# Where a layer's side work is done: sums of output-weight quarters, modulation columns and pauses regrouped between stages of a two-layer backbone

## The chip, the cores and the metric

The kernel runs on one core of a Trainium2 chip. The metric is device time in microseconds (us) of one launch; several launches of the same program are summarised by their median. A profile is of one execution, whose own time stands beside it.

## What is computed

Two layers over 2048 latent tokens of width 1024 in fp32. Layer 0 is a chunked gMLP, layer 1 a multi-scale pooling mixer; the third kind of layer does not occur, and the context tokens are not used. Cut to what matters here:

```python
for i in range(2):
    shift, scale, gate = split(silu(c) @ ada_w[i] + ada_b[i], 3)      # the modulation: 24 columns of 128
    h = rmsnorm(x, norm_g[i]) * (1 + scale) + shift
    if i == 0:
        u, v, g = split(h @ w_in, 3)
        v = layernorm(gelu(v)); s = per-group 128x128 mix of v + b_s   # the spatial gate
        y = (gelu(u) * s * silu(g)) @ w_out
    else:
        p, g = split(h @ w_in, 2)
        y = (group-mixed (centred mean(p) - p) * scale * silu(g)) @ w_out
    x = x + gate * y
return rmsnorm(x, final_g)
```

## The kernel before, in words

**Matrix products.** Every fp32 product is made of three matmuls (`mm3`, lines 105 to 109) on operands split into a high and a low part: ScalarE rounds the high part, VectorE subtracts it (`put`, lines 111 to 114). Larger products use a seven-product scheme on 2x2 blocks, so that weights and activations also have to be added and subtracted block by block. A `Stream` (lines 33 to 60) lists all weight jobs in order: SyncE's queue loads them, `make` splits them, and a consumer keeps three or four pairs made ahead of the one it takes (`st.ahead`).

**Stages.** The span is: fusing two weights of layer 1 (7 to 115 us); then, for each half of the tokens of layer 0, the phase of the values v (`v_phase`, lines 821 to 875; the gate values of the spatial gating), the phase of the units u and gate (`b_phase0`, 927 to 963: eight c, each with a u unit and a gate unit of seven products, and four spatial mixes between), and the output product (`c_pairs` by `c_phase0`, 975 to 1013); then layer 1 with `b_phase1` (1131 to 1163), `c_pairs` again, `b_phase1`, and a last output product. In what follows V(0), B0(0), C0(0), V(1), B0(1), C0(1), B1(0) are these phases in order.

**Side work.** Work that no product of the phase needs at once is a list of small steps in one queue, `side`. `do_side(n)` (118 to 120) runs the next n. `v_phase` calls it after each of its 56 tiles of 12 matmuls: two steps after each of the first eight tiles when it is V(0), one otherwise (line 867). `b_phase0` has 112 calls, one after each product (12 matmuls); `pace` (931 to 933) divides what is left by the calls that are left and rounds up. `b_phase1` runs one step after each product of a first unit and two after each product of a gate unit (line 1161); its own pooling steps go in ahead of the rest. The order of instructions of each engine is fixed when the program is built, by program order and by the builder's own estimate of when each can start; `load` (128 to 131) puts a side load into SyncE's queue behind the stream's last load.

**The side work that the diff touches.**
- `sum_quarters(dst, q)` (732 to 751): `fetch` issues four loads of 256 KB on GpSimd's queue into the tiles x, x, ra, th; `sums` does four subtractions on VectorE (lines 744 to 747; the first is held in program order) and issues four stores on GpSimd's queue. x has two buffers, ra and th one each, so a fetch waits for the stores before. `spaced` (753) makes it fetch, rest, rest, sums, rest: five steps, eight times. `tsum_o` sums the quarters of layer 0's output weight into `to_d`, `tsum` those of layer 1's fused weight into `t_d`, `tsum_p` those of layer 1's output weight into `tp_d`.
- `ada_late(i, *gs)` (468 to 470): for each g four columns of the modulation of layer i, in 14 steps: a first load, eight steps of one 256 KB load into x (SyncE's queue) and one multiply-add on VectorE into ra (lines 452, 454), four rests, and `last`, four small products on TensorE (`pm`, line 460) that need ra. Columns 0 to 15 are shift and scale, 16 to 23 gate.
- `fetched_rms(..., wait)` (544 to 567): eight squares summed over 1024 rows into ra, then `wait` rests, `root` (`pss`, line 502), `wait` rests, `diagonals`, `wait` rests, `spread` (`pr`, line 526): 12 + 3·wait steps.
- `bias_steps` and `late[1]` (769, 818): 12 and 4 steps at the start of V(0).

Where each is needed: `to_d` in C0(0) and C0(1); `tp_d` and layer 1's gate columns in layer 1's first output product; layer 1's shift and scale in C0(1), where B1(0)'s rows are made.

Of the kernel before, what the change touches and what calls it, by code (L numbers as in the profile page):

```python
# [22 lines left out]
TB = 512  # L23
# [40 lines left out]
def hybrid_kernel(ctx: ExitStack, tc: tile.TileContext, a: dict):  # L64
# [29 lines left out]
    def work(tag, width=512):  # L94
        return wk.tile([P, WK[tag][0]], F32, name=tag, tag=tag, bufs=WK[tag][1])[:, 0:width]

    def bank(name="ps"):
        return ps.tile([P, 512], F32, name=name, tag="ps")
# [15 lines left out]
        nc.vector.tensor_sub(pair[1], src, pair[0].bitcast(F32))  # L114

    side = deque()

    def do_side(n=1000):
        for _ in range(min(n, len(side))):
            side.popleft()()  # L120
# [7 lines left out]
    def load(dst, src):  # L128

        with tc.issue_after(st.last):  # L130
            nc.sync.dma_start(dst, src)
# [291 lines left out]
    def ahead(n, fetch, places=2):  # L423

        got = []

        def get(i):
            while len(got) < min(n, i + 1 + places):
                got.append(fetch(len(got)))
            return got[i]  # L430

        return get

    def ada_steps(i, g0, ng, raw, acc_tile):

        box = []
        cols = slice(g0 * P, (g0 + ng) * P)

        def fetch(k):
            r = raw()[:, 0:ng * P]  # L440
            load(r, a["ada_w"][i, k, :, cols])
            return r

        row = ahead(KD, fetch, 1)

        def step(k):
            if k == 0:
                box.append(acc_tile())
            acc = box[0][:, 0:ng * P]
            r = row(k)  # L450
            if k == 0:
                nc.vector.tensor_scalar_mul(acc, r, cond[:, 0:1])
            else:
                nc.vector.scalar_tensor_tensor(acc, r, cond[:, k:k + 1], acc, ALU.mult, ALU.add)

        def last():
            acc = box[0]
            pm = bank("pm")
            for m in range(ng):
                nc.tensor.matmul(pm[:, m:m + 1], acc[:, m * P:(m + 1) * P], ones[:, 0:1], start=True, stop=True)  # L460
            s = slice(g0, g0 + ng)
            nc.vector.tensor_add(mod[i][:, s], pm[:, 0:ng], ada_b[i][:, s])
            if g0 < 16 <= g0 + ng:
                nc.vector.scalar_tensor_tensor(acol[i], mod[i][:, KD:2 * KD], 1.0, norm_g[i], ALU.add, ALU.mult)

        return [partial(row, 0)] + [partial(step, k) for k in range(KD)] + [last]

    def ada_late(i, *gs):
        return [f for g in gs for t in (ada_steps(i, g, 4, lambda: work("x"), lambda: work("ra")),)
                for f in t[:-1] + [rest] * 4 + t[-1:]]  # L470
# [67 lines left out]
    def src0(b):  # L538
        return lambda d: a["xT"][d, :, b * TB:(b + 1) * TB]

    def src1(b):
        return lambda d: x1_d[d, :, b * TB:(b + 1) * TB]

    def fetched_rms(src, n, acc, sq, wait=0, kept=None):

        rms = Rms(n, acc, sq)

        def fetch(d):
            x = work(sq if kept is None else "g", n)
            load(x, src(d))  # L550
            if kept is not None:
                kept.append(x)
            return x

        row = ahead(KD, fetch, 1)

        def step(d):
            x = row(d)
            if d == 0 or kept is not None:
                rms.square(x, d == 0)  # L560
            else:
                nc.scalar.activation(x, x, AF.Square)
                nc.vector.tensor_add(rms.acc, rms.acc, x)

        pause = [lambda: None] * wait
        return rms, ([partial(row, 0)] + [partial(step, d) for d in range(KD)] + pause
                     + [rms.root] + pause + [rms.diagonals] + pause + [rms.spread])
# [4 lines left out]
    class Rows:  # L572
# [9 lines left out]
        def fetch(self, half, d, tile_of):  # L582
            x = tile_of()
            load(x, self.src[half](d))
            return x
# [167 lines left out]
    def spaced(jobs):  # L753
        return [g for fetch, sums in jobs for g in (fetch, rest, rest, sums, rest)]
# [14 lines left out]
    def bias_steps():  # L769

        box = []

        def fetch(q):
            box[:] = [work(tag) for tag in ("x", "x", "ra", "th")]
            nc.gpsimd.dma_start(box[2], a["w_sT"][:, q * 512:q * 512 + 512])
            nc.gpsimd.dma_start(box[3], a["b_s"][:, q * 512:q * 512 + 512].broadcast_to([P, 512]))

        def make(q):
            wsT, bsb = box[2:]
            pw = bank("pw")  # L780
            nc.tensor.matmul(pw, ones, wsT, start=True, stop=True)
            for i in range(2):
                for g in range(2):
                    for h in range(2):
                        c, o = 2 * (4 * q + 2 * i + g) + h, (2 * i + g) * P
                        nc.vector.scalar_tensor_tensor(
                            box[i][:, (2 * g + h) * P:(2 * g + h + 1) * P], pw[:, o:o + P], vb[:, c:c + 1],
                            bsb[:, o:o + P], ALU.mult, ALU.add)
                nc.gpsimd.dma_start(bt_d[4 * q + 2 * i:4 * q + 2 * i + 2].rearrange("g p n -> p g n"),
                                    box[i].rearrange("p (g n) -> p g n", g=2))  # L790

        return [f for q in range(2) for f in (partial(fetch, q), rest, rest, partial(make, q), rest, rest)]
# [6 lines left out]
    rms, steps = fetched_rms(src0(1), TB, "ra", "x", 0, others)  # L799
    rms0.append(rms)  # L800
    late = rows.rest_steps(xb, others)
# [124 lines left out]

    def b_phase0(bb, rows, stats):
        st.ahead = 4
        left = [112]

        def pace():
            left[0] -= 1
            return -(-len(side) // (left[0] + 1))

        fetch, normalise, mix = spatial(bb, stats)
        fetch(0)
        normalise(0)
        for c in range(8):
            gu = [work("g") for _ in range(4)]
            u = unit(rows, jug[bb][c][0], gu, lambda j: nc.scalar.activation(gu[j], gu[j], AF.Gelu_apprx_tanh))  # L940
            for i, pn in enumerate(ORDER):
                u(pn, pace())
                if i == 3:
                    ss = mix(c)
            for j in (0, 2, 3, 1):
                nc.vector.tensor_mul(ss[j], ss[j], gu[j])
            gt = [work("g") for _ in range(4)]

            def gate(j):
                nc.scalar.activation(gt[j], gt[j], AF.Silu)  # L950
                nc.vector.tensor_mul(ss[j], ss[j], gt[j])
                if j != 2:
                    nc.gpsimd.dma_start(y_d[bb, c, (0, 1, None, 3)[j]], ss[j])

            g = unit(rows, jug[bb][c][1], gt, gate)
            for i, pn in enumerate(ORDER):
                g(pn, pace())
                if c < 7 and i == 0:
                    fetch(c + 1)
                if c < 7 and i == 3:  # L960
                    normalise(c + 1)
            side.appendleft(partial(row_sums, bb, c, ss, gt))
        do_side()
# [53 lines left out]
    tsum_p = [sum_quarters(tp_d[k], lambda h, k=k: a["p_wo"][k + 8 * h]) for k in range(8)]  # L1017
    tsum_o = [sum_quarters(to_d[k], lambda h, k=k: a["g_wo"][2 * k + h]) for k in range(8)]


    side.extend(late[1] + bias_steps())
    stats = v_phase(0, rows)
    do_side()
    rms0 = []
    for b in (2, 3):
        rms, steps = fetched_rms(src0(b), TB, "ra", "x", 5)
        rms0.append(rms)
        side.extend(steps)
    side.extend(spaced(tsum_o) + ada_late(0, 16, 20) + ada_late(1, 0, 4, 8))
    b_phase0(0, rows, stats)  # L1030
    rows = Rows(0, [src0(2), src0(3)], rms0)
    sums = rows.sum_steps(lambda: work("g"))
# [7 lines left out]
    do_side()  # L1040
    rms1 = []
    for b in (0, 1):
        rms, steps = fetched_rms(src1(b), TB, "ra", "x", 8)
        rms1.append(rms)
        side.extend(steps)
    side.extend(spaced(tsum_p) + ada_late(1, 12, 16, 20))
    b_phase0(1, rows, stats)
    rows = Rows(1, [src1(0), src1(1)], rms1)
    sums = rows.sum_steps(lambda: work("g"))
# [119 lines left out]
    b_phase1_side = []  # L1169
    rms1 = []  # L1170
    for b in (2, 3):
        rms, steps = fetched_rms(src1(b), TB, "ra", "x", 8)
        rms1.append(rms)
        b_phase1_side += steps
    side.extend(b_phase1_side)
    b_phase1(0, rows)

    rows = Rows(1, [src1(2), src1(3)], rms1)
# [30 lines left out]
    for j, (t0, n) in enumerate(LAST):  # L1209
# [3 lines left out]
        rms = Rms(n, "ra", "x")  # L1213
# [79 lines left out]
```

## Time and profile before

| what | value |
|---|---|
| median of 3 launches | 2444.57 us (2443.26 to 2446.61) |
| the profiled execution's own time | 2441.26 us |
| span in its profile | 2439.5 us |
| TensorE (matmul) busy | 2375.7 us, 97% |
| VectorE busy | 1985.2 us, 81% |
| ScalarE / GpSimd busy | 1091.8 us, 45% / 402.6 us, 17% |
| mean granted TensorE clock | 0.986 |
| mean DMA traffic | 198 GB/s |

The profile cuts the span into 40 slices of 61 us and gives the busy share of each engine in each, the clock that TensorE was granted as a share of 2.4 GHz, and the share of the 16 DMA engines. Other views of the same execution give windows of one's own choice, the instructions of one engine in order of time, who waited for whom, and the chain of work that ended last. Times in them are us from the span's start. In a row of instructions the arrow reads output<-input, and what stands in brackets is the engine's idle time just before and what ended it.

### The profile page before, as it was taken

The numbers are of one execution on the slowest core, as the hardware profiler recorded it, in microseconds if no ns is written. First come the engines' busy times: TensorE is split into PE (matmuls) and PEld (weight loads), VectorE is DVE, ScalarE is ACT, GpSimd is POOL, SyncE is SP. The second block draws the span as 40 slices with busy tenths as digits, with TensorE's granted clock in tenths as the row PEclk, the third lists the DMA queues.
The fourth block names the chain that finished last, engine by engine and source line by source line (L and its number), as shares of the span: only waits on it lengthen the run. The fifth ranks groups of instructions, "written<-read, shape, count | busy, mean of one in ns | idle before, by whom it ended". The sixth has DMA issues, their size and how long they took to land.

```text
span 2439.5 us, 33346 instructions
## 1 busy us (share of the span) xinstructions
PE 2375.7 (97%) x11104; PEld 2000.2 (82%) x11104; DVE 1985.2 (81%) x3323; ACT 1091.8 (45%) x1886; POOL 402.6 (17%) x742
## 2 busy tenths in 40 slices
PE   8999999599999999999999999999999999999998
PEld 7768888488888887888788788888888888888998
DVE  6885887789888786887998878899889688988655
ACT  5743553244465344543445553333356433323533
POOL 2211114300101342014211011121111101000011
PEclk9999999799999999999999999999999999999999
DMA  9733446754678775448657775443378735446764
GB/s 373 248 125 116 159 142 236 241 189 158 209 266 271 242 248 195 142 152 267 232 180 255 245 252 169 138 150 130 120 241 261 252 132 181 142 131 188 225 193 131
DMA packets 204765, 483.41 MB, mean 198 GB/s; under 512 B 27168, under 2 KB 52768, under 8 KB 203568
## 3 DMA queue, kind: packets, MB, share of 16 engines
q1 hardware_dynamic: 152784, 314.00, 40.3%
q0 software_dynamic: 47776, 162.52, 18.9%
q10 hardware_dynamic: 4032, 4.75, 0.7%
q8 instruction: 88, 1.44, 0.3%
q14 instruction: 85, 0.70, 0.1%
HBM read 356.47 MB, written 124.70 MB: 197 GB/s over the span
## 4 chain that ended last, share of the span: by engine, by line
PE 67%; DMA 7%; DVE 5%; issue 4%; POOL 1%; ACT 0%; SPq 0%; POOLq 0%; DVEq 0%; ACTq 0%
PE pu L107 14%; PE pu L109 13%; PE pu L108 13%; PE po L109 7%; PE po L107 7%; PE po L108 7%; DVE wlo L114 2%; PE psp L907 1%; PE pa L109 1%; PE pa L108 1%; PE pa L107 1%; DMA x<-in_g_wo 1%; DMA raw<-to_d 1%; DMA x<-x_d 1%; DMA raw<-in_g_wo 1%
## 5 line engine op out<-in xcount | busy, mean ns | idle before, releaser
L113 ACT CAST whi<-raw 128x512 fp32r<-128x512 f32 (+1 forms) x960 | 562.9, 617 | 596.2 <-PE pu L108 225.8
L114 DVE TENSOR_TENSOR wlo<-raw,whi 128x512 fp32r<-128x512 f32 (+1 forms) x960 | 631.7, 683 | 127.9 <-ACT whi L113 125.0
L107 PE MATMUL pu<-S,whi 128*128 128x512 f32 x1024 | 403.4, 394 | 14.7 <-DVE g L695 8.1
L109 PE MATMUL pu<-S,wlo 128*128 128x512 f32 x1024 | 401.2, 392 | 0.7 <-DVE wlo L114 0.7
L108 PE MATMUL pu<-S,whi 128*128 128x512 f32 x1024 | 401.0, 392 | 0.0
L107 PE MATMUL pu<-A,whi 128*128 128x512 f32 x768 | 301.8, 393 | 0.0
L109 PE MATMUL pu<-A,wlo 128*128 128x512 f32 x768 | 300.0, 391 | 0.0
L108 PE MATMUL pu<-A,whi 128*128 128x512 f32 x768 | 299.8, 390 | 0.0
L109 PE MATMUL po<-whi,wlo 128*128 128x512 f32 (+1 forms) x672 | 262.6, 391 | 3.5 <-DVE wlo L114 3.4
L107 PE MATMUL po<-whi 128*128 128x512 f32 (+1 forms) x672 | 261.8, 390 | 0.0
L108 PE MATMUL po<-wlo,whi 128*128 128x512 f32 (+1 forms) x672 | 261.6, 389 | 0.0
L107 PEld LDWEIGHTS pu<-S,whi 128*128 128x128 f32 x1024 | 193.7, 189 | 55.8 <-DVE g L695 9.3
L109 PEld LDWEIGHTS pu<-S,wlo 128*128 128x128 f32 x1024 | 193.6, 189 | 42.2 <-DVE wlo L114 1.6
L108 PEld LDWEIGHTS pu<-S,whi 128*128 128x128 f32 x1024 | 193.9, 189 | 39.6
L109 PEld LDWEIGHTS pu<-A,wlo 128*128 128x128 f32 x768 | 144.7, 188 | 30.6
L108 PEld LDWEIGHTS pu<-A,whi 128*128 128x128 f32 x768 | 145.0, 189 | 29.8
L107 PEld LDWEIGHTS pu<-A,whi 128*128 128x128 f32 x768 | 145.1, 189 | 29.6
L109 PEld LDWEIGHTS po<-whi,wlo 128*128 128x128 f32 x672 | 126.1, 188 | 33.2 <-DVE wlo L114 7.3
L108 PEld LDWEIGHTS po<-wlo,whi 128*128 128x128 f32 x672 | 126.2, 188 | 26.5
L107 PEld LDWEIGHTS po<-whi 128*128 128x128 f32 x672 | 126.2, 188 | 26.0
L107 PE MATMUL po<-big,whi 128*128 128x388 f32 (+1 forms) x384 | 123.2, 321 | 0.0
L108 PE MATMUL po<-big,whi 128*128 128x388 f32 (+1 forms) x384 | 122.8, 320 | 0.0
(261 smaller groups left out, 4075.6 us busy)
## 6 DMA issues: line engine op xcount, KB each, us to landing
raw<-in_p_wo SPq DMA_DIRECT2D x120, 256.0 KB, 3.5
raw<-y_d SPq DMA_DIRECT2D x112, 256.0 KB, 3.7
v_d<-g POOLq DMA_DIRECT2D x64, 256.0 KB, 3.0
raw<-in_g_wu SPq DMA_DIRECT2D x32, 512.0 KB, 4.4
raw<-in_g_wg SPq DMA_DIRECT2D x32, 512.0 KB, 4.4
raw<-v_d SPq DMA_DIRECT2D x32, 512.0 KB, 4.7
y_d<-s POOLq DMA_DIRECT2D x64, 256.0 KB, 3.3
x<-in_ada_w SPq DMA_DIRECT2D x64, 256.0 KB, 3.3
```

The lines of the kernel that those rows point to most:

```text
L107: nc.tensor.matmul(out, w[0], x[0], start=first and not onto, stop=False, skip_group_check=onto)
L108: nc.tensor.matmul(out, w[0], x[1], start=False, stop=False, skip_group_check=onto)
L109: nc.tensor.matmul(out, w[1], x[0], start=False, stop=last, skip_group_check=onto)
L113: nc.scalar.copy(pair[0], src)
L114: nc.vector.tensor_sub(pair[1], src, pair[0].bitcast(F32))
L907: nc.tensor.matmul(p[:, t * P:(t + 1) * P], vt[h][:, t * 2 * P + j * P:t * 2 * P + (j + 1) * P], bw[:, 0:P], start=True, stop=True)
```

## The change

The closure `pace` becomes a function `evenly`, with the same arithmetic. `tsum_o` (40 steps) goes from B0(0) to V(0), behind the 16 steps that were there. Of the modulation of layer 1, columns 8 to 11 go from B0(0) to B0(1), and columns 16 to 23 from B0(1) to B1(0). The four `fetched_rms` for layer 1's rows that ran with pauses of 8 rests get 5.

```diff
+    def evenly(places):
+
+        left = [places]
+
+        def pace():
+            left[0] -= 1
+            return -(-len(side) // (left[0] + 1))
+
+        return pace
...
     def b_phase0(bb, rows, stats):
         st.ahead = 4
-        left = [112]
-
-        def pace():
-            left[0] -= 1
-            return -(-len(side) // (left[0] + 1))
-
+        pace = evenly(112)
...
-    side.extend(late[1] + bias_steps())
+    side.extend(late[1] + bias_steps() + spaced(tsum_o))
     stats = v_phase(0, rows)
...
-    side.extend(spaced(tsum_o) + ada_late(0, 16, 20) + ada_late(1, 0, 4, 8))
+    side.extend(ada_late(0, 16, 20) + ada_late(1, 0, 4))
     b_phase0(0, rows, stats)
...
     for b in (0, 1):
-        rms, steps = fetched_rms(src1(b), TB, "ra", "x", 8)
+        rms, steps = fetched_rms(src1(b), TB, "ra", "x", 5)
...
-    side.extend(spaced(tsum_p) + ada_late(1, 12, 16, 20))
+    side.extend(spaced(tsum_p) + ada_late(1, 8, 12))
     b_phase0(1, rows, stats)
...
     for b in (2, 3):
-        rms, steps = fetched_rms(src1(b), TB, "ra", "x", 8)
+        rms, steps = fetched_rms(src1(b), TB, "ra", "x", 5)
...
-    side.extend(b_phase1_side)
+    side.extend(b_phase1_side + ada_late(1, 16, 20))
     b_phase1(0, rows)
```

Steps per phase, by counting the lists (without the eight `row_sums` of a B0 phase, which are put in front): V(0) 16 before and 56 after, B0(0) 164 and 110, B0(1) 154 and 122, B1(0) 72 and 82 (beside its own pooling and gating steps).

## Rows read from the trace of the kernel before

**Rows 1.** The page, busy tenths and granted clock in 40 slices of 61 us

```profile
PE   8999999599999999999999999999999999999998
PEclk9999999799999999999999999999999999999999
```

**Rows 2.** Windows of B0(0), B0(1), B1(0), V(0), V(1): PE, PEld, DVE, ACT, POOL, clock, DMA, GB/s

```profile
278.49:658.20 379.71, 350.06 (x1668) 293.25 (x1666) 316.42 (x549) 153.68 (x251) 68.11 (x120) 0.96 0.58 189
966.94:1313.42 346.48, 342.07 (x1652) 288.14 (x1650) 307.38 (x538) 151.05 (x253) 69.49 (x122) 0.99 0.59 197
1470.42:1778.99 308.57, 308.57 (x1378) 256.02 (x1377) 273.16 (x422) 105.82 (x179) 54.46 (x136) 1.00 0.46 146
...
114.93:278.65 163.72, 158.21 (x678) 127.22 (x677) 125.39 (x217) 82.29 (x143) 29.65 (x42) 0.99 0.39 129
811.99:967.10 155.11, 153.45 (x674) 126.09 (x673) 111.54 (x184) 68.95 (x119) 58.04 (x99) 1.00 0.68 227
```

**Rows 3.** Window of 20 us inside B0(0), same columns

```profile
460.00:480.00 20.00, 5.28 (x24) 4.04 (x22) 17.39 (x31) 2.40 (x4) 3.79 (x7) 0.69 0.69 233
```

**Rows 4.** Timeline of PE: start, us, engine, line, out<-in, idle before and its end

```profile
431.26 0.79 PE L107 MATMUL pu<-S,whi 128*128 128x512 f32 x1 [6.55 <-DVE g L690]
...
483.91 0.59 PE L460 MATMUL pm<-ones,ra 128*128 128x1 f32 x2 [18.63 <-DVE ra L454]
...
1161.98 0.79 PE L107 MATMUL pu<-S,whi 128*128 128x512 f32 x1 [4.41 <-DVE g L695]
```

**Rows 5.** Chain that ended last, B0(0): start, us, what

```profile
424.25 7.59 DMA to_d<-x
...
432.40 3.80 DMA x<-in_g_wo
...
466.52 3.98 DMA x<-in_ada_w
```

**Rows 6.** Timeline of DVE: first and last of eight first subtractions in B0(0), V(1), B0(1)

```profile
372.36 0.68 DVE L744 TENSOR_TENSOR x<-x 128x512 f32<-128x512 f32 x1
...
460.32 0.69 DVE L744 TENSOR_TENSOR x<-x 128x512 f32<-128x512 f32 x1 [1.91 <-DMA x<-in_g_wo]
...
820.65 0.69 DVE L744 TENSOR_TENSOR x<-x 128x512 f32<-128x512 f32 x1 [2.69 <-issue]
...
920.21 0.69 DVE L744 TENSOR_TENSOR x<-x 128x512 f32<-128x512 f32 x1 [6.15 <-issue]
...
1088.44 0.68 DVE L744 TENSOR_TENSOR x<-x 128x512 f32<-128x512 f32 x1
...
1190.31 0.68 DVE L744 TENSOR_TENSOR x<-x 128x512 f32<-128x512 f32 x1
```

**Rows 7.** Chain that ended last, later in B0(0): the modulation's small products

```profile
530.30 0.79 PE pm L460 x8
...
572.93 0.79 PE pm L460 x8
```

**Rows 8.** Modulation steps, 484 to 658 us: duration min/median/max; then their waits: total, times, longest

```profile
L454 DVE SCALAR_TENSOR_TENSOR ra<-x,cond,ra x28: 737/744/752, 489.4 to 639.3; 128x512 f32<-128x512 f32 x28
...
DVE ra L454 <- DMA x<-in_ada_w: 2.1, 3, 0.8
```

**Rows 9.** Windows: early V(0), what follows, V(1) to 930 us, c = 4 to 6 of B1(0)

```profile
135.00:155.00 20.00, 15.88 (x58) 11.71 (x59) 19.78 (x39) 7.25 (x11) 4.11 (x6) 0.91 0.24 79
155.00:197.00 42.00, 41.64 (x181) 33.19 (x180) 33.37 (x60) 21.61 (x39) 9.11 (x13) 1.00 0.52 179
...
811.99:930.00 118.01, 118.01 (x522) 97.77 (x521) 86.00 (x138) 49.17 (x83) 51.37 (x89) 1.00 0.73 245
...
1624.70:1740.41 115.71, 115.71 (x520) 96.07 (x519) 103.49 (x160) 37.12 (x61) 20.25 (x42) 1.00 0.38 127
```

**Rows 10.** Instructions on the tensor to_d: ns min/median/max, first and last start

```profile
L749 POOL DMA_DIRECT2D to_d<-x x16: 539/544/548, 373.8 to 462.5; - x16
```

**Rows 11.** Timeline of PE: a mean-square round with nothing beside it, at the end

```profile
2431.77 1.22 PE L526 MATMUL pr<-ra,ones 128*128 128x128 f32 x4 [2.17 <-DVE ra L518]
```

## Prediction, made before the changed kernel was run

> **What bounds the kernel now.** I read the page first. TensorE is nine tenths busy or more in every slice but the first, the last and the eighth, which holds 427 to 488 us: five tenths there, and a granted clock of 0.7 [rows 1]. So the kernel is bound by TensorE, and what can still be won without taking products away is idle time and time at the lower clock. The windows cut at phase borders show where it is: B0(0) takes 379.71 us with TensorE busy in 350.06 of them; B0(1), with the same products, takes 346.48 with 342.07 busy; B1(0) has no idle time at all [rows 2].
>
> Then the timeline of TensorE in B0(0). The idle 29.65 us (379.71 − 350.06) are a few gaps, all between 424 and 484 us. The two largest are 6.55 us, ended by VectorE's g of line 690, and 18.63 us, ended by VectorE's sum ra of line 454, for which the small product pm stood waiting at the head of TensorE's order [rows 4]. In the 20 us that hold most of the second the clock was 0.69 of 2.4 GHz, so TensorE was part of the time at its 1.2 GHz level [rows 3].
>
> Last, the chain that ended last, to see why VectorE was late. It runs through the sums of to_d in a circle: a store to_d<-x landed after 7.59 us, only then the next load x<-in_g_wo could be issued (3.80 us), then the subtractions and again the stores; after the last store, the first modulation load into the same tile x came (3.98 us) [rows 5]. One turn of this circle took (460.32 − 372.36)/7 = 12.6 us [rows 6]. `pace` had asked for more: 164 steps over 112 calls is two a call at first, five steps make 2.5 calls, and a call is worth 3.05 us (below), so a turn was placed every 7.6 us. VectorE takes its work in order; each turn that was 5 us late held up the splits and the product sums behind it, until the pairs made ahead were used up and TensorE stopped.
>
> What an undisturbed c of B0 costs is read from the same phase once the sums are over: the small products pm come at 530.30 and 572.93 us, one c apart, so a c takes 42.63 us and a call 42.63/14 = 3.05 us [rows 7]. Eight of them are 341.0 us. B0(0) loses 379.71 − 341.0 = 38.7 us, 29.65 as idle time and about 9 as lower clock; B0(1) loses 346.48 − 341.0 = 5.4 us, 4.41 of it one gap [rows 2, 4].
>
> **The change part by part.**
>
> *B0(0): tsum_o leaves, and one modulation round.* 110 steps remain for 112 calls, so all goes at one a call. The mean-square steps had run at two a call before 360 us without any gap; at one they have more time. The four modulation rounds left go at one a call as the four after 484 us did, where VectorE waited 2.1 us in all for their loads and TensorE not at all [rows 8]. I take the whole 38.7 us back: **−38.7** (bounds −38.7 and −30: the one gap that I would not exclude is one of the size left in B0(1), 4.41 with its share of clock, twice). The small products weigh about the same: four pm rounds and two mean-square rounds against one pm of 0.79 us in each of the eight c that I used [rows 7].
>
> *V(0): tsum_o arrives.* All of it counts: 32 loads and 32 stores of 256 KB on GpSimd's queue, 32 subtractions. V(1) is the nearest case, with the eight turns of tsum at one step a tile and nothing else: a turn every (920.21 − 820.65)/7 = 14.2 us, TensorE busy in all of the 118.01 us up to 930 us, which hold all eight turns [rows 6, 9], and 155.11 us for the phase with 1.7 idle after them [rows 2]. Its DMA engines were busy 0.68 of the time against 0.39 in V(0) now, so the added transfers fit too [rows 2]. On GpSimd's queue the v stores pass between the fetches in V(1) just as they will here. What differs is the start: from 135 to 155 us VectorE is busy 19.78 of 20 us with late[1], the bias steps and the block differences, and TensorE already idles there; from 155 to 197 us it has 33.37 of 42 [rows 9]. The first `sums` falls at the twelfth tile, about 150 us: its four subtractions, 4·0.69 = 2.8 us [rows 6], have no room and go straight onto TensorE's path. The later seven have. **+2.8** (0 if the builder slips them into the waits; 8 if two turns and a load of 3.8 us [rows 5] show).
>
> A rule speaks against putting these transfers beside a busier VectorE. What the row shows: GpSimd's issue of a to_d store took 539 to 548 ns, over all sixteen, with VectorE nearly full [rows 10]; nothing held it. The Trainium skill ("SBUF — State Buffer", "Who interferes with whom") says that GpSimd and a VectorE instruction in a two-port mode exclude each other for a whole instruction, and gives about 620 ns alone against 3100 ns overlapped for a transfer issued by GpSimd. By that rule each turn's eight issues would cost 8·2.5 = 20 us more of GpSimd's queue, an estimate from that page, and the sum would be rival D's loss. By the row it stays as it is, and I go by the row.
>
> *B0(1): one modulation round fewer, pauses of 5.* 122 steps instead of 154: two a call only for the first ten calls, so all eight turns of tsum_p run at one a call, 5·3.05 = 15.2 us apart. Before, the first two ran closer and the mean was (1190.31 − 1088.44)/7 = 14.6 us [rows 6], so this changes little, and the turns fall at the same products of a c as before, one c later. The 4.41 us gap [rows 4] has even odds to come back. **−2.7**, half of 5.4 (bounds −5.4 and 0).
>
> *B1(0): two gate rounds arrive.* By counting steps they run in c = 4, 5, 6. VectorE is busy 103.49 of 115.71 us there [rows 9]; sixteen multiply-adds at 0.744 us are 11.9 us [rows 8]: 115.4 of 115.7. It fits, barely; four pairs made ahead, four products of about 2.75 us (308.57/112 [rows 2]), cover 11 us of lag. Two pm rounds are 1.6 us of TensorE. For lag I take the 2.0 us that the modulation's own load waits added up to in B0(0) [rows 8]: **+3.6** (bounds 1.6, and 14 if each of 16 steps waits 0.8 us).
>
> *Pauses 8 to 5.* In B1(0) five rests are 2.5 calls of 2.75 us, about what B0(0) gave its mean squares at two a call, where TensorE did not wait: 0. What hides them is that stretch of products. Were it gone, each of four rounds would cost about twice the 2.17 us of a round with nothing beside it [rows 11]: 17 at worst.
>
> *evenly* is the same arithmetic: 0.
>
> **Sum**: −38.7 + 2.8 − 2.7 + 3.6 = −35.0. The profiled execution took 2441.26 us, 3.3 below the median of 2444.57; against it the changed kernel comes to 2406.3, against the median to **2409.6 us**.
>
> **The rivals.**
>
> *B, VectorE becomes the bound in B1(0).* For it: 115.4 of 115.7 us. Then the gate steps' waits of up to 0.8 us each cannot be caught up, and pm, fixed in TensorE's order, waits as it did at 483.91 us [rows 4, 8]. 14 instead of 3.6 gives 2420. Against: c = 7 has no such steps and eleven us of cover stand before. Chance 0.14.
>
> *C, the large gap stays.* The 18.63 us wait was for modulation, not for sums [rows 4]. If SyncE's queue, not the tile, made those loads late, it returns with the first gate round of B0(0): 18.63/29.65 of 38.7 is 24.3, giving 2433.9. Against: the chain leads from the store of to_d into that load [rows 5], and four later rounds had no gap. Chance 0.08.
>
> *D, slower.* Place: V(0); mechanism: GpSimd's queue. If a turn there takes longer than its five tiles, VectorE stands at line 744 in every turn, as in B0(0), and TensorE with it: per turn 2.8 us of subtractions and up to a 3.8 us load are exposed, and the late store of 7.59 us less the slack moves every next one [rows 5]. Eight turns at 2.8 + 7.59 are 83 us, giving 2490. It decides from 35/8 = 4.4 us beyond my 2.8 shared by all, that is when a turn takes over about 18 us. Against: V(1)'s turns took 14.2 us where five tiles are 5·153.45/56 = 13.7, and cost TensorE nothing [rows 2, 6, 9]. The Trainium skill's rule on GpSimd and VectorE, above, would bring this about; the row of 539 to 548 ns bears it out in no part. Chance 0.05.
>
> *E, no change.* The order of each engine is fixed by the builder's estimates, only the first subtraction is pinned; if V(0) loses what B0(0) wins, or the late circle is the modulation's, the time stays 2444.6. Chance 0.04.
>
> **How the numbers follow.** The forecast has the remaining 0.69; its own range is 2401 (B0(0) and B0(1) fully restored, nothing lost in V(0) or B1(0) but pm: −42.5, and a little more) to 2418. The range given reaches over B: 2399 to 2427, leaving out C, D and E, 0.17. A measurement of this kernel tells about 0.2%, 4.9 us, from no change. Faster: the forecast, B and C, 0.91; same: E, 0.04; slower: D, 0.05.
>
> **What would show it.** In the changed profile: the eighth slice at nine tenths and a clock of 1.00; B0(0) at 341 to 346 us with no pm gap above 2 us; eight subtractions of line 744 in V(0) between 150 and 265 us, 13 to 15 us apart; V(0) at 164 to 170 us; B1(0) at 310 to 314 us with VectorE above 110 of 116 us in c = 4 to 6. I am wrong if B0(0) stays above 355 us, if V(0) exceeds 175, or if B1(0) shows gaps at pm.

## The result, and the profile after

The changed kernel takes 2402.27 us (median of 4 launches, 2398.14 to 2404.24) against 2443.91 us for the kernel before (4 launches, 2440.51 to 2446.61). The ratio is 0.9828 with a 95% interval of 0.981 to 0.9846: 1.7% faster, by 41.6 us. The prediction was 2409.6 us, 35 us faster, with a range of 2399 to 2427. The profiled execution took 2402.30 us, its span is 2400.5 us, 39.0 less than before.

First the page of the changed kernel: busy tenths of TensorE and its granted clock in 40 slices (each 60 us now), to be read against [rows 1].

```profile
PE   8999999999999999999999999999999999999998
PEclk9999999999999999999999999999999999999999
```

The eighth slice is like its neighbours: no idle half, no low clock. Then the windows cut at the same phase borders (start:end, length, busy us and instructions of PE, PEld, DVE, ACT, POOL, then clock, DMA share, GB/s): V(0), B0(0), C0(0), B0(1), C0(1), B1(0) and layer 1's first output product C1.

```profile
114.53:278.28 163.75, 158.44 (x678) 127.31 (x677) 138.53 (x240) 77.64 (x134) 64.69 (x106) 0.99 0.65 222
278.12:620.36 342.24, 340.87 (x1660) 287.36 (x1658) 296.89 (x516) 159.00 (x259) 33.84 (x56) 1.00 0.50 159
621.01:776.88 155.87, 153.65 (x675) 126.06 (x675) 129.51 (x211) 89.03 (x156) 17.32 (x33) 1.00 0.79 265
...
931.41:1269.77 338.36, 338.36 (x1644) 285.52 (x1642) 302.54 (x529) 152.75 (x253) 69.49 (x122) 1.00 0.59 195
1270.42:1428.02 157.60, 154.93 (x675) 127.29 (x675) 125.42 (x205) 88.77 (x155) 17.25 (x32) 0.99 0.75 247
1427.85:1738.32 310.47, 310.47 (x1394) 257.77 (x1393) 281.96 (x440) 103.93 (x179) 52.12 (x136) 1.00 0.50 158
1738.16:1894.27 156.11, 154.71 (x674) 125.70 (x673) 126.42 (x204) 89.86 (x157) 21.40 (x37) 1.00 0.82 258
```

The three output products did not stand among the rows of before, so here they are from the kernel before, same columns and order:

```profile
658.85:812.15 153.30, 152.91 (x675) 126.33 (x675) 129.43 (x211) 89.09 (x156) 17.27 (x33) 1.00 0.80 269
1314.07:1470.59 156.52, 153.53 (x675) 126.15 (x675) 125.96 (x205) 88.94 (x155) 17.27 (x32) 1.00 0.76 249
1778.82:1933.22 154.40, 154.26 (x674) 125.88 (x673) 126.20 (x204) 89.69 (x157) 21.39 (x37) 1.00 0.83 261
```

Where the time came from, after minus before, with [rows 2] for the phases that stood there:

| phase | before | after | difference | forecast |
|---|---|---|---|---|
| V(0) | 163.72 | 163.75 | 0.0 | +2.8 |
| B0(0) | 379.71 | 342.24 | −37.5 | −38.7 |
| C0(0) | 153.30 | 155.87 | +2.6 | 0 |
| V(1) | 155.11 | 154.87 | −0.2 | 0 |
| B0(1) | 346.48 | 338.36 | −8.1 | −2.7 |
| C0(1) | 156.52 | 157.60 | +1.1 | 0 |
| B1(0) | 308.57 | 310.47 | +1.9 | +3.6 |
| C1 | 154.40 | 156.11 | +1.7 | 0 |

The rest (fusion, B1(1), the last product) differs by 0.1 us or less each. The growth of the three output products is of the size by which single executions differ: over this kernel and the eleven of the experiments, none of which touches a line of theirs, they took 154.4 to 156.4, 154.4 to 159.3 and 154.5 to 156.8 us, with no order in it. The execution of before lies below all twelve in the first and the third; that this is scatter is likely, and not shown.

Two rows of the changed kernel's timelines show what became of the two waits of [rows 4]. On VectorE, the first and the last first subtraction of tsum_o, now in V(0); on TensorE, the one gap left in B0(0) and the first small product pm:

```profile
168.00 0.69 DVE L754 TENSOR_TENSOR x<-x 128x512 f32<-128x512 f32 x1 [2.51 <-DMA x<-in_g_wo]
...
264.75 0.67 DVE L754 TENSOR_TENSOR x<-x 128x512 f32<-128x512 f32 x1
```

```profile
290.42 0.38 PE L917 MATMUL psp<-bw,raw 128*128 128x128 f32 x1 [1.26 <-DVE raw L908]
...
492.29 0.50 PE L470 MATMUL pm<-ones,ra 128*128 128x1 f32 x4
```

A turn in V(0) takes (264.75 − 168.00)/7 = 13.8 us, which is five tiles; pm has no bracket, so TensorE did not wait for it.

### The profile page after: what moved, and what is told of

The parts are those of the page before. It is cut to its first block, busy times and chain, and to the rows that moved or that the text cites. A ratio compares the mean times of both kernels' runs of the same rounds, so it can differ in the third digit from the quotient of the medians.

```text
span 2400.5 us, 33322 instructions
## 1 busy us (share of the span) xinstructions
PE 2367.3 (99%) x11104; PEld 1994.1 (83%) x11104; DVE 1982.4 (83%) x3323; ACT 1093.0 (46%) x1886; POOL 400.2 (17%) x742
## 4 chain that ended last, share of the span: by engine, by line
PE 80%; DMA 7%; DVE 6%; issue 4%; POOL 1%; ACT 1%; SPq 1%; DVEq 0%; POOLq 0%; ACTq 0%
PE pu L107 17%; PE pu L109 17%; PE pu L108 17%; PE po L109 7%; PE po L107 7%; PE po L108 7%; PE psp L917 2%; DVE wlo L114 2%; DMA xb<-in_xT 1%; PE pa L107 1%; PE pa L108 1%; PE pa L109 1%; DMA g<-x_d 1%; DMA raw<-to_d 1%; PE pv L107 1%
## 5 line engine op out<-in xcount | busy, mean ns | idle before, releaser
L109 PEld LDWEIGHTS po<-whi,wlo 128*128 128x128 f32 x672 | 126.5, 188 | 37.5 <-DVE wlo L114 11.1
```

The source lines that it names most:

```text
L109: nc.tensor.matmul(out, w[1], x[0], start=False, stop=last, skip_group_check=onto)
```

## The experiments

The theory put to the test is one of pace: a turn of the sums needs 11 to 14 us for its circle of loads, subtractions and stores, and where the steps ask for one more often, VectorE falls behind and TensorE stops. Its first rival says that the place matters (a unit phase has no room for these sums), its second that the modulation is to blame for the large wait. Where only one launch is named, the time is that launch's; phase lengths are always those of one profiled execution. How well a phase repeats can be read from the runs that left it alone: B0(0) took 379.71 and 379.30 us, and B0(1) 346.48, 346.15, 345.55 and 348.23 us.

**Each half of the change alone.** First, only the sums moved:

```diff
-    side.extend(late[1] + bias_steps())
+    side.extend(late[1] + bias_steps() + spaced(tsum_o))
...
-    side.extend(spaced(tsum_o) + ada_late(0, 16, 20) + ada_late(1, 0, 4, 8))
+    side.extend(ada_late(0, 16, 20) + ada_late(1, 0, 4, 8))
```

> Only tsum_o goes to V(0); the modulation's rounds and the pauses stay as before. Theory (rate: a turn of the sums takes 12 to 14 us by its own circle of loads and stores, B0(0) asked for one every 7.6 us): B0(0) falls from 379.7 to 341 to 346 us, V(0) stays at 164 to 167, B0(1) stays near 346 with one gap of some 4 us; the time is about 2406. Rival (the large gap was the modulation's own): B0(0) stays above 355, the time above 2420.

2406.48 us (4 launches), ratio 0.9846 (0.983 to 0.9861). B0(0), then B0(1), and the one gap in the latter:

```profile
276.82:620.83 344.01, 341.82 (x1668) 288.29 (x1666) 301.69 (x526) 158.49 (x259) 33.92 (x57) 1.00 0.51 165
932.24:1278.39 346.15, 342.38 (x1652) 288.40 (x1650) 307.69 (x539) 150.86 (x253) 69.64 (x122) 0.99 0.60 197
```

```profile
1126.64 0.80 PE L107 MATMUL pu<-S,whi 128*128 128x512 f32 x1 [3.77 <-DVE g L695]
```

As the theory had it; V(0) stayed at 163.75 us. Then the other half, the kernel after with tsum_o put back into B0(0):

```diff
-    side.extend(late[1] + bias_steps() + spaced(tsum_o))
+    side.extend(late[1] + bias_steps())
...
-    side.extend(ada_late(0, 16, 20) + ada_late(1, 0, 4))
+    side.extend(spaced(tsum_o) + ada_late(0, 16, 20) + ada_late(1, 0, 4))
```

> tsum_o stays in B0(0); the modulation's rounds and the pauses are as in the changed kernel. Theory (rate): B0(0) stays within 5 us of 379.7, with the wait at the small product pm; B0(1) 338 to 341 as in the changed kernel, B1(0) about 310.5; the time is 2434 to 2442. Rival (modulation): B0(0) falls to 365 or less, since one modulation round fewer stands behind the sums.

2412.62 us (4 launches), ratio 0.9873 (0.9856 to 0.9889): a clear miss of what I expected. With the sums still in B0(0) the phase shrank to 355.22 us. The window, and from TensorE's timeline the two gaps of the turns and the first pm:

```profile
275.80:631.02 355.22, 345.15 (x1660) 290.27 (x1658) 309.49 (x540) 150.49 (x251) 68.11 (x120) 0.98 0.60 196
```

```profile
427.94 0.79 PE L107 MATMUL pu<-S,whi 128*128 128x512 f32 x1 [5.92 <-DVE g L700]
...
436.94 0.79 PE L107 MATMUL pu<-S,whi 128*128 128x512 f32 x1 [4.15 <-DVE g L705]
...
502.95 0.39 PE L470 MATMUL pm<-ones,ra 128*128 128x1 f32 x3
```

The gaps of the turns are still there, the wait at pm is gone. So the loss of B0(0) has two parts, and the halves of the change do not add up: −35.7 us in B0(0) from the first, −24.5 from the second, −37.5 from both. The rival's number (365 or less) came true, but it can be the work that was moved or the number of steps that is left: 150 in place of 164 means two steps a call for some 38 calls instead of some 52, and the last turns and the first modulation round fall behind that point.

**Pace or place.** tsum_o in B0(0), but ten steps a turn:

```diff
-    side.extend(ada_late(0, 16, 20) + ada_late(1, 0, 4))
+    side.extend([g for fetch, sums in tsum_o for g in (fetch, *[rest] * 5, sums, *[rest] * 3)]
+                + ada_late(0, 16, 20) + ada_late(1, 0, 4))
```

> tsum_o stays in B0(0), but with ten steps a turn in place of five, so that a turn gets five calls (15.2 us) at two steps a call; all else as in the changed kernel. Theory (rate): B0(0) is 341 to 352 us, no wait at pm above 3 us, and the time is within 10 us of the changed kernel's 2402. Rival (place: a unit phase cannot take these sums at all, because VectorE, GpSimd's queue or the transfers are full there): B0(0) stays above 360 us and the time above 2420.

2404.38 us (4 launches), ratio 0.9838 (0.9823 to 0.9854), which overlaps that of the changed kernel. B0(0), and the one gap in it:

```profile
277.96:624.89 346.93, 343.60 (x1660) 289.47 (x1658) 309.66 (x540) 150.38 (x251) 68.23 (x120) 0.99 0.60 199
```

```profile
516.32 0.56 PE L470 MATMUL pm<-ones,ra 128*128 128x1 f32 x2 [3.32 <-DVE ra L464]
```

Inside the theory's range but for 0.3 us at pm. A unit phase can take the sums; the rival of place falls. The other way round, the changed kernel with its sums pressed together in V(0):

```diff
-    side.extend(late[1] + bias_steps() + spaced(tsum_o))
+    side.extend(late[1] + bias_steps() + [f for t in tsum_o for f in t])
```

> The changed kernel with the sums in V(0) at two steps a turn and no rests: a turn every two tiles, 5.5 us. Theory (rate): the circle of 12 to 14 us shows in V(0) as well; eight turns need some 100 us where 44 are placed, less the pairs made ahead, so V(0) grows from 163.8 to 180 to 215 us. Rival (place: V(0) has the room, whatever the pace): V(0) stays below 170 us.

2411.01 us (one launch). V(0), and the first and last first subtraction:

```profile
114.37:289.48 175.11, 162.91 (x678) 129.18 (x677) 139.46 (x242) 77.66 (x140) 63.72 (x105) 0.97 0.61 210
```

```profile
168.11 0.69 DVE L754 TENSOR_TENSOR x<-x 128x512 f32<-128x512 f32 x1 [2.77 <-DMA x<-in_g_wo]
...
243.76 0.69 DVE L754 TENSOR_TENSOR x<-x 128x512 f32<-128x512 f32 x1 [2.13 <-issue]
```

The turns could not be had at 5.5 us: they came every (243.76 − 168.11)/7 = 10.8 us, the circle's own length when nothing else spaces it. V(0) grew by 11.4 us, with a clock of 0.97. The direction is the theory's, the size (16 to 51 us were expected) is not: V(0) bears a late turn better than I worked out.

**What the wait at pm hangs on.** Two edits of the kernel before, neither of which moves any work between phases. Fourteen rests ahead of the first pm:

```diff
-    side.extend(spaced(tsum_o) + ada_late(0, 16, 20) + ada_late(1, 0, 4, 8))
+    first = ada_late(0, 16)
+    side.extend(spaced(tsum_o) + first[:-1] + [rest] * 14 + first[-1:] + ada_late(0, 20) + ada_late(1, 0, 4, 8))
```

> The kernel before, with fourteen rests more in front of the small products of B0(0)'s first modulation round; the sums stay where and as fast as they were. Theory (two losses: the turns stop TensorE by some 10 us of gaps and 4 of slow clock, and pm, fixed in TensorE's order seven calls behind the last turn, by 18.6 us and some 6 of clock): the wait at the first pm falls from 18.6 to under 4 us and B0(0) from 379.7 to 353 to 360 us. Rival (the modulation's loads are late by themselves): the wait at pm stays above 10 us, B0(0) above 368.

2432.04 us (one launch, beside 2440.31). B0(0), and the gaps with the first pm:

```profile
276.00:644.56 368.56, 350.67 (x1668) 293.25 (x1666) 314.84 (x549) 151.48 (x251) 68.33 (x120) 0.97 0.59 195
```

```profile
428.17 0.80 PE L107 MATMUL pu<-S,whi 128*128 128x512 f32 x1 [5.94 <-DVE g L690]
...
437.46 0.79 PE L107 MATMUL pu<-S,whi 128*128 128x512 f32 x1 [4.84 <-DVE g L695]
...
472.10 0.71 PE L107 MATMUL pu<-A,whi 128*128 128x512 f32 x1 [4.46 <-ACT whi L113]
...
493.28 0.39 PE L460 MATMUL pm<-ones,ra 128*128 128x1 f32 x3
```

The wait at the first pm is gone, so the loads were not late by themselves. But the phase is longer than I expected (368.56 us, which is the rival's figure for the phase, though its wait at pm is not there): a new gap of 4.46 us stands where pm no longer does, at a weight split. The lateness had only been taken where it showed first. And the same with 18 empty steps less, pauses of 2 in the two mean-square rounds:

```diff
-        rms, steps = fetched_rms(src0(b), TB, "ra", "x", 5)
+        rms, steps = fetched_rms(src0(b), TB, "ra", "x", 2)
```

> The kernel before with pauses of 2 instead of 5 in B0(0)'s two mean-square rounds: 18 steps fewer, all of them empty, so that the modulation's rounds come at one step a call while the sums still come at two; no work is moved. Theory (step count: what took the wait at pm away in the run with tsum_o left in B0(0) was the pace of the first modulation round, not the round that was gone): no wait at pm above 4 us, B0(0) 348 to 360 us, the time 2408 to 2424. Rival (the modulation round that was moved mattered as work): the wait at pm stays above 12 us and B0(0) above 370.

2428.34 us (one launch, beside 2443.68 for the median of before). B0(0), its two largest gaps and the first pm:

```profile
276.50:642.76 366.26, 351.76 (x1668) 292.99 (x1666) 315.26 (x549) 149.87 (x251) 68.57 (x120) 0.97 0.59 196
```

```profile
390.75 0.50 PE L107 MATMUL pu<-S,whi 128*128 128x512 f32 x1 [3.45 <-DVE g L695]
...
423.12 0.80 PE L107 MATMUL pu<-A,whi 128*128 128x512 f32 x1 [3.26 <-ACT whi L113]
...
472.06 0.39 PE L460 MATMUL pm<-ones,ra 128*128 128x1 f32 x3
```

Again no wait at pm, though all the work is where it was: not the moved round but the count of steps decides it. The length was missed again (366 for at most 360), since the sums now start nine calls earlier and seven of the eight turns come at two steps a call; TensorE stops six times between 387 and 456 us, for 0.4 to 3.5 us, and once before, for 1.7 us at the pss of the second shortened mean-square round.

Counting in the traces how many products of B0(0) (12 matmuls each) stand ahead of the last turn's first subtraction and ahead of the first pm puts the five runs in one line:

| run | last turn after | first pm after | between | wait at the first pm |
|---|---|---|---|---|
| before | 54.3 | 56.0 | 1.8 | 18.6 us |
| ten steps a turn | 70.3 | 77.0 | 6.7 | 3.3 us |
| pm 14 steps later | 54.3 | 63.0 | 8.8 | 0 |
| pauses of 2 | 45.2 | 56.0 | 10.8 | 0 |
| second half alone | 57.9 | 70.0 | 12.1 | 0 |

A modulation round takes 17.4 us from its first load to its pm (466.52 to 483.91 [rows 4, 5]). Its first load waits for the last stores of the sums and starts 6.2 us after the last turn's first subtraction (460.32 [rows 6]). Together that is 23.6 us, eight to nine products at 2.7 us, and pm's place among the products is fixed; what is missing between the two is TensorE's wait.

**The pauses and B0(1).** The kernel before with only this edit, for the two mean-square rounds of B0(1):

```diff
-        rms, steps = fetched_rms(src1(b), TB, "ra", "x", 8)
+        rms, steps = fetched_rms(src1(b), TB, "ra", "x", 5)
```

> The kernel before with pauses of 5 instead of 8 in B0(1) and nothing else: all eight turns of tsum_p come at one step a call, the last five at the same calls as before. Theory (pace: the gap of 4.4 us comes from the first two turns, asked for at two steps a call, whose lateness is handed on): B0(1) falls from 346.5 to 338 to 341 us. Rival (place: what collides with the fifth and sixth turn at the border of c = 3 and 4): the gap stays and B0(1) is 345 to 348 us.

2433.0 us (one launch, beside 2440.31). B0(1):

```profile
965.75:1305.11 339.36, 339.36 (x1652) 286.47 (x1650) 307.43 (x539) 151.70 (x253) 69.48 (x122) 1.00 0.61 201
```

No gap is left, although the last five turns fall on the same calls as before: what stopped TensorE at the sixth was lateness handed on from the turns ahead of it, which had been asked for at two steps a call. The sixth turn ran after 62.1 products before and after 59.4 here. But it is not the pauses that count:

```diff
-        rms, steps = fetched_rms(src1(b), TB, "ra", "x", 5)
+        rms, steps = fetched_rms(src1(b), TB, "ra", "x", 8)
```

> The changed kernel with pauses of 8. Theory (pace): B0(1) keeps all turns at one step a call and stays at 338 to 341 us; in B1(0) the gate columns now come in c = 5 to 7 and their last small products at the very end, which costs B1(0) 0 to 6 us; the time is 2400 to 2410. Rival (the pauses of 5 brought B0(1)'s gain): B0(1) is 345 us or more.

With that edit in the changed kernel, in all four rounds: 2401.03 us (one launch), B0(1) 338.42 and B1(0) 309.52 us. And with pauses of 1 in the same places:

> The changed kernel with pauses of 1 in the four rounds of layer 1. Theory (the pauses hide a chain of small steps from TensorE): up to twice 2.2 us a round show, B0(1) and B1(0) grow by 3 to 9 us each. Rival (the builder's order and the pairs made ahead hide it anyway): both phases stay within 1 us of 338.4 and 310.5.

2399.38 us (one launch), B0(1) 339.32 and B1(0) 312.65 us, with two small gaps in B1(0) (0.3 and 1.4 us) at pss and pr. B0(1) has no gap; it is longer by one pm round of 0.95 us, which otherwise falls just past its last product (and B1(0) with pauses of 8 is shorter by one for the same reason). So one rest in place of five costs B0(1) nothing, as the rival said, and B1(0) some 2 us, less than the theory's 3, and eight or five are the same. What the pauses set is how many steps are left, and so whether the turns behind them come at one step a call.

**A version faster than both.** V(0) still loses 9 us against V(1), all before 158 us, where VectorE is full and the steps have just run at two a tile for eight tiles. One step a tile, first with late[1] ahead of the bias steps:

```diff
-                    do_side(2 if pb == n == 0 and pn < 3 else 1)
+                    do_side(1)
...
-    side.extend(late[1] + bias_steps() + spaced(tsum_o))
+    side.extend([f for s in late[1] for f in (s, rest)][:-1] + bias_steps()[:-2] + spaced(tsum_o)[:-1])
```

> The changed kernel with one step a tile in all of V(0), late[1] on every second of its first seven tiles, then the bias steps, then the sums. Theory (VectorE is full at the start of V(0), and the doubled pace there makes the gaps of 1.3 and 3.1 us with their slow clock): V(0) falls from 163.8 to 157 to 161 us. Rival (the gaps come from the backlog of the fusion's end, whatever the pace): V(0) stays within 1 us of 163.8.

2399.91 us (4 launches), ratio 0.9823 (0.9806 to 0.9839). V(0) 158.45 us as expected, but B0(0) 348.27, with a wait at its first spatial product that the changed kernel has at 1.26 us:

```profile
288.02 0.55 PE L917 MATMUL psp<-bw,raw 128*128 128x128 f32 x1 [5.34 <-issue]
```

Then both kinds of step alternating over sixteen tiles:

```diff
-    side.extend(late[1] + bias_steps() + spaced(tsum_o))
+    b = [f for f in bias_steps() if f is not rest]
+    side.extend([f for p in zip(b, late[1]) for f in (*p, rest, rest)] + spaced(tsum_o)[:-1])
```

> As the run before, but late[1] and the bias steps alternate, two steps in four tiles, over the first sixteen tiles. Theory: V(0) 155.5 to 160 us, at most as long as in the run before. Rival (backlog): V(0) within 1 us of 163.8.

2390.01 us (4 launches, 2389.13 to 2392.47), ratio 0.9782 (0.9768 to 0.9797): 2.2% under the kernel before and clear of the changed kernel's interval. V(0) and B0(0) together are 10.0 us shorter than in the changed kernel, all of the 9.8 us between the two profiled executions (2402.30 and 2392.47); the medians lie 12.3 us apart. V(0), B0(0), and the 20 us that were worst in [rows 9]:

```profile
113.66:269.36 155.70, 155.51 (x678) 126.80 (x677) 136.28 (x238) 78.58 (x135) 60.59 (x99) 1.00 0.63 213
269.20:609.50 340.30, 340.30 (x1660) 287.31 (x1658) 298.70 (x520) 157.56 (x259) 37.66 (x64) 1.00 0.52 170
...
135.00:155.00 20.00, 19.82 (x82) 14.74 (x81) 20.00 (x39) 9.03 (x16) 5.23 (x8) 1.00 0.34 106
```

VectorE is as full there as it was (20.00 of 20 us), and TensorE hardly waits: it was the order of VectorE's work, not its amount.

Why the first spatial product waits in the one version and not in the other can be read from VectorE's timeline. The last turn now falls at the start of B0(0), and its first subtraction stands in VectorE's order just ahead of the scaling of v (line 908) that the spatial product needs. First the version with late[1] ahead, then the alternating one:

```profile
286.90 0.69 DVE L754 TENSOR_TENSOR x<-x 128x512 f32<-128x512 f32 x1 [3.19 <-DMA x<-in_g_wo]
287.51 0.41 DVE L908 TENSOR_SCALAR raw<-raw,mv,rs 128x256 f32<-128x256 f32 x1
```

```profile
277.25 0.69 DVE L754 TENSOR_TENSOR x<-x 128x512 f32<-128x512 f32 x1
277.86 0.41 DVE L908 TENSOR_SCALAR raw<-raw,mv,rs 128x256 f32<-128x256 f32 x1
```

In the one VectorE stands 3.19 us at the turn, waiting for its load, and the scaling with it; in the other the load is there in time. It is a late turn once more. Why the load was later in the one was not followed further.

## Why the prediction was right

**B0(0), −38.7 forecast, −37.5 measured.** Right in size. The floor that I read from one later c (341.0 us) is confirmed by the last version, whose B0(0) has no idle time and takes 340.30. The mechanism was right too, the circle of loads and stores against a pace of 2.5 calls a turn; the runs with slow turns in B0(0) and fast ones in V(0) show it. My length for a turn, 12.6 us, was a mean: five of the seven were 10.4 to 12.0 us, the other two 15.9 and 17.1. What I had not seen is that the loss was two things, the turns' own stops and the wait at pm, and that most of the gain could be had without moving the sums at all: 24.5 us of this phase by the run with the other half alone, 32.8 us with ten steps a turn. I had set the step "tsum_o leaves" down as the only cause and the dropped modulation round as a thing of no weight. The size came out all the same because I had taken the phase down to its floor, whatever the parts of the loss were; to that extent it was luck.

**V(0), +2.8 forecast, 0.0 measured.** The bound "0 if the builder slips them into the waits" was the right end. The first turn did not come at 150 us but at 168.00, behind the full stretch, since GpSimd's queue had the fetch stand behind the stores of the bias steps. VectorE's busy time rose by 13.1 us only (125.39 to 138.53), though the 32 subtractions are some 22. Part of the rest, 4.1 us, is mean-square additions that the builder had drawn ahead into V(0), seven before and one now; the others run in B0(0). GpSimd's issues of the stores were not held up by VectorE, which was busy 37.04 of 42 us from 155 to 197 us while the turns kept their 13.8 us:

```profile
L759 POOL DMA_DIRECT2D to_d<-x x16: 540/554/580, 169.0 to 267.4; - x16
```

[rows 10] do not show a VectorE nearly full, as I had read them: from 373 to 463 us of the kernel before it was busy 64.94 of 90 us. The Trainium skill ("SBUF — State Buffer", "Who interferes with whom") also says that `tensor_tensor` has no two-port mode. The turns' subtractions are of that kind, so the rule that I quoted from there was not one for them, and the row agrees. The 620 and 3100 ns stand in another section of that page ("A bandwidth-pool intuition that's wrong (but worth ruling out)") and are for a `tensor_copy`.

**B0(1), −2.7 forecast, −8.1 measured.** The most mis-sized term, by 5.4 us. Two errors. I gave the gap even odds because the turns fall on the same products of a c as before; the run with pauses of 5 alone has no gap, so the handed-on lateness of the first turns decided it, and one step a call for all was a sure gain. And my floor was 2.6 us high: 341.0 holds eight pm rounds of 0.95 us, where the phase now holds one (its second falls just past the last product) and two mean-square rounds of 2.0 us. That comes to 338.4, and it measures 338.36.

**B1(0), +3.6 forecast, +1.9 measured.** Exactly the two pm rounds, 0.95 us each here. VectorE had no lag: the row for c = 4 to 6, to be read against the last of [rows 9], is

```profile
1582.13:1697.84 115.71, 115.71 (x524) 96.15 (x523) 109.91 (x166) 35.87 (x61) 18.75 (x42) 1.00 0.47 151
```

109.9 of 115.7 us, where I had worked out 115.4. The sixteen steps all fell into that window, from 1584.7 to 1669.1 us, and took 11.4 us. What I had not taken off is that other work left it: with shorter pauses the root and the diagonals of the second mean-square round, some 1.9 us, came earlier, and a few of the phase's own operations now fell outside. TensorE was busy throughout. Rival B is out.

**Pauses, 0 forecast.** Right for five against eight; one instead of five shows some 2 us in B1(0) and nothing in B0(1).

**The sum, −35.0 forecast, −39.0 between the profiled executions, −41.6 between the medians.** The four phases gave 43.7 us, 8.7 more than forecast; the three output products, put at nothing, took back 5.4 in these executions. That the two misses run against each other is luck.

**The other rivals.** C said that SyncE's queue makes the modulation late; with room ahead of pm the wait is gone, so it does not, but C's doubt, that the large wait was not the sums' alone, had more in it than its 0.08. D, V(0) turning slower than the gain: even at the pace of two tiles a turn V(0) lost 11.4 us, not 38. E: the builder did not undo the move.

## What to carry to other kernels

Side work has a pace of its own: a step list that loads, computes and stores through the same few buffers cannot turn faster than that circle (here 10.8 us in the mean when nothing else spaced it), and asking for more makes the in-order engine late for the work that matters. So look at how many steps a phase divides over how many calls: dropping empty steps or moving unrelated ones can bring a list from two a call to one, and that is where both halves of this change won. And when a late chain ends in an instruction with a fixed place in the bound engine's order, read the distance between the two in the trace; moving only that instruction shifts the stop to the next one in line.

## What the runs showed that I had not expected

The halves of the change do not add: 37.5 and 31.3 us by the medians alone (2443.96 to 2406.48 and to 2412.62), 41.6 together. VectorE was busy 20.00 of 20 us at the start of V(0) in the last version and TensorE still had 19.82: a full engine off the bound one's path cost next to nothing once its work came in the right order. And V(0) took turns that were late by half their length, 10.8 for 5.5 us, for 11.4 us in all, where B0(0) lost 38.7 with a smaller shortfall, 12.6 for 7.6; but 18.6 of these were the wait at pm, and V(0) has no such small product behind its turns.
